# Sums of squares by ones times split parts, a summed last square, warm-up matmuls and a later epilogue in a two-layer decoder step

## The chip, the cores and the metric

The kernel runs on one core of a Trainium2 chip. The time is that of one execution on the device, in microseconds (us). The engines are PE (matrix products, with PEld for loading their stationary operand), DVE (vector operations), ACT (functions and copies), POOL and SP (the last two mostly issue transfers). Each works through its own row of instructions in order and waits on semaphores of the others.

## The reference

One step of a decoder trunk with two layers on 512 new tokens and 8 sequences of 4 tokens, 544 tokens of 1024 channels, all fp32:

```python
def rmsnorm(x, g):
    return x * lax.rsqrt(jnp.mean(x * x, axis=-1, keepdims=True) + EPS) * g

def trunk_layer(x, ...):
    x = x + 0.5 * swiglu(rmsnorm(x, g_ffn1), w_ffn1_up, w_ffn1_down)
    z = rmsnorm(x, g_mix) @ w_in
    ...                                   # three mixers: chunked gate, short convolution, pooling
    x = x + merged @ w_o
    x = x + 0.5 * swiglu(rmsnorm(x, g_ffn2), w_ffn2_up, w_ffn2_down)
    x = x + sigmoid(rmsnorm(x, g_ple) @ w_ple_gate) * (p @ w_ple_proj)
y = rmsnorm(x, g_final)
```

So there are four norms in a layer and one at the end, nine in all. The pooling mixer multiplies its output with a factor per channel (`c_scale`).

## The kernel before

**Data.** Channels lie on the 128 partitions, tokens along the free dimension: x is eight tiles of 128x544. A product of fp32 values is made of three PE passes over values split into a high and a low part in a reduced fp32 form (`split_to`: ACT copies the high part, DVE subtracts it for the low part). A matmul covers half of the tokens, 272 columns.

**Order of the work.** The program is written out as one stream, and each engine gets its instructions in the order of the source. Weights come in units of 128x512, which are loaded, added and split a few units ahead of their use. Each new unit calls `tick`, which also runs deferred steps: `later` is a list of steps with a number of ticks to wait, `background` a list that is spread over ticks, and `flush` runs all of both at once. PSUM has four tiles ps71 to ps74 of two banks, which `bank` and `ring_bank` hand out in turn by the counter `psi`.

**Products.** `gemm` (L303) is the plain form. `s_pair` (L326) computes two outputs with seven products on sums of blocks in place of eight; each of its products is 12 matmuls. It works in banks X, Y, Z, V: the products go to X, Y, X, Z, X, V, X, and X is copied out (L586, L588, L593) before it is filled again. A feed-forward (`ffn`, `ff_group`) makes its first output group by `gemm` (the program's very first four groups) and the others by `s_pair`. The epilogue of a plain group (`fin`) has the steps `e0` (gate times the norm's scale, L643), `dz` (Silu on ACT), `e1` (up times gate, L646), `dr`, `d2`, `d3`.

**Norms.** Each new block of x is squared on ACT and added to `acc` (`sumsq`, L385 to L389). While the products that follow already run on x without the scale, `rms_hooks` inserts the norm: `rms_sum` (L521) multiplies 128 tokens of `acc` at a time with a column of ones, which gives the sums as columns with a token per partition; DVE and ACT make the inverse root on these (`inv_sqrt`: Sqrt on ACT, the rest on DVE) and put them on diagonals (L528); `rms_bc` (L535) multiplies ones with the diagonals, which brings the scale to all partitions; ACT copies it to `rstd` (L537, L539). `RMS_AT` says after how many pieces of the first group of products (6 matmuls each) the two parts stand. Functions of ACT belong to tables, and a function of another table has an ACT_TABLE_LOAD ahead of it.

**End.** `ple_last` does the last sublayer in two parts of the tokens, blocks 0 to 1 and blocks 2 to 4 (256 and 288 columns), so that the first part's final norm and outputs lie under the second part's products (`gate`, `proj`: L1110). The last norm of all follows the last product.

Of the kernel before, what the change touches and what calls it, by code (L numbers as in the profile page):

```python
# [9 lines left out]
F32R = mybir.dt.float32r  # L10
# [33 lines left out]
N_PLAIN = 4  # L44
RMS_AT = 7, 14
V_TICKS = 9
RMS_AT0 = 8, 1
LAST_AT = 12, 26
TOK0 = T - P

GN_FFN1, GN_MIX, GN_FFN2, GN_PLE = range(4)
# [52 lines left out]
class Kern:  # L104
    def __init__(self, nc, ins, outs, sb, pp, plan=None):
        self.nc, self.ins, self.outs = nc, ins, outs
        self.sb = sb
        self.dry = plan is None
        self.seq, self.use = ([], [0]) if self.dry else plan
        self.used = 0  # L110
        self.held = ()
        self.keep = False
        self.extra = 0
        self.names = 0

# [9 lines left out]
        self.ones = self.mk([P, P], "ones")  # L125
        self.par = self.mk([P, PB_N], "par")
# [375 lines left out]
    def tok0(self, i):  # L502
        return i * P if i < 4 else TOK0

    def inv_sqrt(self, v, s, r, t):
        nc = self.nc
        nc.scalar.activation(s, v, AF.Sqrt)
        nc.vector.reciprocal(r, s)
        nc.vector.tensor_mul(t, r, r)
        nc.vector.tensor_mul(t, t, v)  # L510
        nc.vector.tensor_scalar(t, t, -0.5, 1.5, op0=ALU.mult, op1=ALU.add)
        nc.vector.tensor_mul(r, r, t)
# [4 lines left out]
    def rms_sum(self, ps, i0=0, i1=5):  # L517
        nc = self.nc
        for i in range(i0, i1):
            t0 = self.tok0(i)  # L520
            nc.tensor.matmul(ps[:, i:i + 1], self.acc[:, t0:t0 + P], self.ones[:, 0:1], start=True, stop=True)  # L521
        v, s, r, t = (self.cols[:, o + i0:o + i1] for o in (0, 8, 16, 24))
        nc.vector.tensor_scalar(v, ps[:, i0:i1], 1.0 / D, EPS, op0=ALU.mult, op1=ALU.add)
        self.inv_sqrt(v, s, r, t)
# [17 lines left out]
    def rms_hooks(self, then=None):  # L542
        st = {}
        start, self.start = self.start, False

        def first():
            st["ps"], = self.bank(1)
            self.rms_sum(st["ps"][:, 0, :])
            if start:
                self.later.append((RMS_AT0[1], second))  # L550

        def second():
            self.rms_bc(st["ps"])
            if then:
                self.background(*then)

        if start:
            self.later.append((RMS_AT0[0], first))
            return ()
        return tuple(zip(RMS_AT, (first, second)))  # L560

    def scaled(self, ps):
        t = self.slot()
# [40 lines left out]
    def ff_group(self, up, l, j, inp, first, plain, hs, hsl):  # L604
        nc = self.nc
        t_, o_ = self.slot(), self.slot()
        t, o = t_[0], o_[0]
        a, b = self.rpair()
        hi, lo = a[0][:, :], b[0][:, :]
        hs.append((hi, lo))  # L610
        hsl.extend((a, b))

        def dz():
            nc.scalar.activation(t[:, :], t[:, :], AF.Silu)  # L614

# [12 lines left out]

        def dr():
            nc.vector.tensor_mul(o[:, :], o[:, :], self.rstd[:, :])  # L630

        if plain:
            start = self.start
            xg = inp.tiles
            pg, pu = self.gemm([(up, l, j, xg, 0), (up, l, NFF + j, xg, 0)], kouter=first,
                               hooks=self.rms_hooks() if first else ())

            def s0():
                nc.scalar.activation(self.v2(t[:, :]), self.pv(pg), AF.Copy)
                nc.scalar.activation(self.v2(o[:, :]), self.pv(pu), AF.Copy)  # L640

            def e0():
                nc.vector.tensor_mul(self.v2(t[:, :]), self.pv(pg), self.v2(self.rstd[:, :]))  # L643

            def e1():
                nc.vector.tensor_mul(self.v2(o[:, :]), self.pv(pu), self.v2(t[:, :]))  # L646

            if start:
                fin = (s0,) + (None,) * (sum(RMS_AT0) - 5) + (d0, dz, d1, dr, d2, d3)
            else:  # L650
                fin = (e0, dz, e1, dr, d2, d3)
        else:
            r = self.rstd
            self.s_pair(up, l, NFF + j, j, inp.sets, o_, t_,
                        lambda out, ps: nc.vector.tensor_mul(out, ps, r[:, HT:]))
            nc.vector.tensor_mul(t[:, :HT], t[:, :HT], r[:, :HT])  # L656
            fin = (dz, dr, d1, d2, d3)
        self.later += [(1 + i, f) for i, f in enumerate(fin) if f]

    def ffn(self, l, which, inp, nxt, tail=None):  # L660
# [18 lines left out]
        for n in FF_PARTS:  # L679
            hs, hsl = [], []  # L680
            items = len(todo)
            for i in range(n):
                j = j0 + i
                self.extra = EXTRA[0] if j < plain else EXTRA[7]
                if j == plain:
                    self.flush()
                    self.drop(*inp.zs)
                self.ff_group(up, l, j, inp, j == 0, j < plain, hs, hsl)
# [39 lines left out]
    def mix(self, l, inp, nxt):  # L728
# [69 lines left out]
            self.split_later(b_, yb, yb_s, 1)  # L798

        self.extra = EXTRA[2]  # L800
        pc, px = self.gemm([W(Z_C), W(Z_XB)], kouter=True, hooks=self.rms_hooks(then=(steps, V_TICKS)))
        conv_in(0, self.scaled(pc), conv_x(0, px))
        def row(name):
            t = self.slot()
# [19 lines left out]
        def v_stat():  # L824
            cv = mv[:, :, 2]
            nc.vector.tensor_scalar_add(cv, mv[:, :, 1], EPS)
            self.inv_sqrt(cv, mv[:, :, 3], mv[:, :, 4], mv[:, :, 5])

        def v_norm(i):
            t = vt[i][:, :SEQ]  # L830
# [131 lines left out]
        def c_mix():  # L962
            for i, j in enumerate(reversed(range(G))):
                pc, = self.gemm([("c_w", l, 0, pooled[j], j)])
                t_ = self.slot()
                o = PB_CS + l * G + j
                nc.vector.tensor_scalar_mul(self.v2(t_[0][:, :]), self.pv(pc), self.par[:, o:o + 1])
                self.drop(*pooled_s[j])
                self.split_later(t_, yc, yc_s, 1 + i)
            yc.reverse()  # L970
# [124 lines left out]
    def ple_last(self, l, inp):  # L1095
# [35 lines left out]
        def proj(h, m):  # L1131
# [7 lines left out]
                nc.scalar.activation(self.acc[:, c], x, AF.Square)  # L1139
            else:  # L1140
                nc.scalar.activation(t, x, AF.Square)
                nc.vector.tensor_add(self.acc[:, c], self.acc[:, c], t)
            self.drop(t_)

        def norm_sum(h):
            rms[h], = self.bank(1)
            self.rms_sum(rms[h][:, 0, :], *parts[h])

        def norm_bc(h):
            self.rms_bc(rms[h], *parts[h])  # L1150

        def out(h, m):
            c = span(h)
# [24 lines left out]
        for m in range(KD):  # L1178
            if m + 1 < KD:
                gate(1, m + 1)  # L1180
            if m == 1:
                norm_sum(0)
            if m == 2:
                norm_bc(0)
            proj(1, m)
            if 2 <= m < 6:
                out(0, 2 * m - 4)
                out(0, 2 * m - 3)
        norm_sum(1)
        norm_bc(1)  # L1190
        for m in range(KD):
            out(1, m)

    def run(self):
        nc = self.nc
        nc.gpsimd.memset(self.ones[:, :], 1.0)
        nc.gpsimd.affine_select(self.ident[:, :], self.ones[:, :], pattern=[[1, P]], compare_op=ALU.is_equal,
                                fill=0.0, base=0, channel_multiplier=-1)
        def gain(l, which):
            return lambda m: self.gain(l, which, m)  # L1200

# [111 lines left out]
```

## Time and profile before

| | us |
|---|---|
| median of three runs | 2421.4 (2421.24 to 2422.02) |
| profiled execution, its time | 2421.51 |
| its span, first to last instruction | 2419.8 |
| PE busy in it | 2395.4 |
| mean granted clock of PE | 0.997 of full speed |

The span is what the trace covers; the execution's own time is 1.7 us longer. The views used below are the page's shares, the waits (who waited for whom), the chain (followed back from the last instruction to whatever released each step), the timeline (instructions in order of time, like ones merged), windows (busy time and clock in a stretch) and the groups by line. A record of an fp32 matmul appears twice, since PE runs it in two.

### The profile page before, as it was taken

What the parts mean: (1) busy time and instruction counts of PE and PEld (TensorE: products, weight loads), DVE (VectorE), ACT (ScalarE), POOL (GpSimd) and SP (SyncE); (2) the same over time, 40 slices, a digit from 0 to 9 for tenths busy, and PEclk for the clock granted to TensorE, in tenths of its full rate; (3) what the DMA queues carried; (4) which work ended last, traced back from release to release, by engine and by line L of the source; (5) the groups of instructions that cost most, each with busy time, mean ns of one, the idle gap of its engine ahead of it and who ended that gap; (6) DMA issues with size and microseconds to landing.
All of it is one profiled execution on the core that took longest, in us unless ns stands there. A gap on an engine that the chain in (4) does not pass through costs nothing.

```text
span 2419.8 us, 48050 instructions
## 1 busy us (share of the span) xinstructions
PE 2395.4 (99%) x18848; PEld 2381.8 (98%) x18848; DVE 1856.7 (77%) x3439; ACT 1208.4 (50%) x2355; POOL 225.6 (9%) x276
## 2 busy tenths in 40 slices
PE   8999999999999999999999999999999999999997
PEld 8999999999999999999999999999999999999997
DVE  7776777877878777778777777778779778867675
ACT  6444444655555544445554444556455555544452
POOL 1101000111100110100010110001111001101000
PEclk9999999999999999999999999999999999999998
DMA  6655561666554555555255554526565536556521
GB/s 205 143 146 140 145 170 40 176 151 153 145 140 121 140 147 147 146 139 160 60 142 135 145 155 126 166 63 173 137 157 154 161 79 153 154 126 154 145 75 38
DMA packets 180034, 329.78 MB, mean 136 GB/s; under 512 B 20256, under 2 KB 22560, under 8 KB 179808
## 3 DMA queue, kind: packets, MB, share of 16 engines
q1 hardware_dynamic: 141264, 255.92, 34.1%
q0 software_dynamic: 36672, 68.51, 16.9%
q8 instruction: 148, 2.42, 0.4%
q10 hardware_dynamic: 1872, 2.29, 0.3%
q14 instruction: 78, 0.64, 0.1%
HBM read 323.64 MB, written 2.99 MB: 135 GB/s over the span
## 4 chain that ended last, share of the span: by engine, by line
PE 97%; DVE 2%; ACT 1%; issue 0%; DMA 0%; DVEq 0%; ACTq 0%
PE ps L326 52%; PE ps L303 39%; PE ps L1110 2%; PE ps L846 2%; PE ps L535 0%; PE ps L521 0%; PE ps L995 0%; DVE s L250 0%; ACT L614 0%; DMA par<-in_par 0%; DVE s L1155 0%; DVE s L630 0%; DVE s L646 0%; PE ps L997 0%; DVE s L369 0%
## 5 line engine op out<-in xcount | busy, mean ns | idle before, releaser
L326 PE MATMUL ps<-s,s 128*128 128x272 f32 x10332 | 1311.2, 289 | 3.4 <-ACT s L586 1.9
L326 PEld LDWEIGHTS ps<-s,s 128*128 128x128 f32 x10332 | 1301.7, 189 | 5.2 <-ACT s L586 2.9
L303 PE MATMUL ps<-s,s 128*128 128x272 f32 x7536 | 962.7, 289 | 7.3 <-ACT s L448 7.3
L303 PEld LDWEIGHTS ps<-s,s 128*128 128x128 f32 x7536 | 952.2, 189 | 7.2 <-ACT s L448 7.2
L250 DVE TENSOR_TENSOR s<-s,s 128x512 fp32r<-128x512 f32 x1211 | 812.0, 685 | 20.1 <-ACT s L245 19.0
L245 ACT ACTIVATE s<-s 128x512 fp32r<-128x512 f32 x1211 | 705.2, 622 | 224.7 <-DVE s L238 222.2
L232 POOL DMA_DIRECT2D s<-in_wts x246 | 210.8, 877 | 1948.4 <-DMA s<-in_wts 717.0
L586 ACT ACTIVATE s<-ps 128x272 f32<-128x272 f32 x123 | 48.8, 397 | 461.7 <-PE ps L326 455.9
L669 DVE SCALAR_TENSOR_TENSOR x<-ps,x 128x544 f32<-128x544 f32 x128 | 92.7, 724 | 184.4 <-PE ps L303 182.6
L238 DVE TENSOR_TENSOR s<-s,s 128x512 f32<-128x512 f32 x246 | 168.6, 685 | 0.0
L589 DVE TENSOR_TENSOR s<-ps,s 128x272 f32<-128x272 f32 x123 | 54.3, 441 | 109.7 <-ACT s L588 109.1
L588 ACT ACTIVATE s<-ps 128x272 f32<-128x272 f32 x123 | 48.7, 396 | 100.4 <-PE ps L326 99.9
L593 ACT ACTIVATE s<-ps 128x272 f32<-128x272 f32 x123 | 48.6, 395 | 89.7 <-PE ps L326 89.4
L594 DVE TENSOR_TENSOR s<-ps,s 128x272 f32<-128x272 f32 x123 | 54.3, 441 | 49.5 <-ACT s L593 48.7
L620 ACT ACTIVATE s<-s 128x544 fp32r<-128x544 f32 x88 | 57.8, 657 | 37.2 <-DVE s L617 21.2
L888 DVE TENSOR_TENSOR s<-ps,s 128x544 f32<-128x544 f32 x48 | 34.8, 724 | 46.8 <-PE ps L303 43.2
L623 DVE TENSOR_TENSOR s<-s,s 128x544 fp32r<-128x544 f32 x88 | 63.4, 720 | 6.0 <-ACT s L620 5.8
L614 ACT ACTIVATE s<-s 128x544 f32<-128x544 f32 x88 | 57.8, 657 | 19.7 <-DVE s L656 18.0
L1110 PE MATMUL ps<-s,s 128*128 128x256 f32 (+1 forms) x480 | 63.2, 294 | 1.8 <-ACT rstd L537 1.8
L1110 PEld LDWEIGHTS ps<-s,s 128*128 128x128 f32 x480 | 62.0, 193 | 2.0 <-ACT rstd L537 2.0
L630 DVE TENSOR_TENSOR s<-s,rstd 128x544 f32<-128x544 f32 x88 | 63.4, 720 | 0.1
L617 DVE TENSOR_TENSOR s<-s,s 128x544 f32<-128x544 f32 x82 | 58.9, 719 | 0.4
(137 smaller groups left out, 1150.1 us busy)
## 6 DMA issues: line engine op xcount, KB each, us to landing
s<-in_wts SPq DMA_DIRECT2D x965, 256.0 KB, 3.3
s<-in_wts POOLq DMA_DIRECT2D x246, 256.0 KB, 5.1
x<-in_xT SPq DMA_DIRECT2D x4, 272.0 KB, 4.9
x<-in_xT ACTq DMA_DIRECT2D x4, 272.0 KB, 5.2
s<-in_pT POOLq DMA_DIRECT2D x4, 272.0 KB, 4.4
out_yT<-s SPq DMA_DIRECT2D x4, 144.0 KB, 1.8
out_yT<-s ACTq DMA_DIRECT2D x4, 144.0 KB, 1.8
s<-in_st_in POOLq DMA_DIRECT2D x2, 272.0 KB, 2.9
```

Of the source, the lines that this page charges most:

```text
L232: self.nc.gpsimd.dma_start(out=t, in_=src(1 if w == "R1" else 2, 4), accum_op=ALU.add)
L238: self.nc.vector.tensor_add(self.new_raw(w, u0, 2 if w == "R3" else 1), self.read_raw(a, u0), self.read_raw(b, u0))
L245: self.nc.scalar.activation(a[0][:, :UC], self.read_raw(w, u0), AF.Copy)
L250: self.nc.vector.tensor_sub(lo, self.read_raw(w, u0), hi.bitcast(F32))
L303: self.nc.tensor.matmul(ps[:, h, :HT], a, bh, start=first and i == 0, stop=last and i == 2)
L326: self.nc.tensor.matmul(ps, a, b, start=first and i == 0, stop=last and i == 2, skip_group_check=go_on)
L614: nc.scalar.activation(t[:, :], t[:, :], AF.Silu)
L617: nc.vector.tensor_mul(o[:, :], o[:, :], t[:, :])
L623: nc.vector.tensor_sub(lo, o[:, :], hi.bitcast(F32))
L630: nc.vector.tensor_mul(o[:, :], o[:, :], self.rstd[:, :])
L669: nc.vector.scalar_tensor_tensor(xm, self.pv(pst[i]), 0.5, xm, op0=ALU.mult, op1=ALU.add)
L1110: nc.tensor.matmul(ps, a, b[:, c], start=first and i == 0, stop=last and i == 2)
```

## The change

Seven norms take a new form. `norm_split` splits `acc` into high and low parts, `norm_sum` multiplies a full matrix of ones with both, so that the sums of squares come out on all partitions at once, and `norm_scale` makes the inverse root there: ACT's Abs_reciprocal_sqrt, then one correcting step (square on ACT, three operations on DVE). These are the norms of both feed-forwards but not of the mixers, of the gated embedding, and the final one: six in the first group of products, the last in two halves. The mixers' norms, which also need the scale as columns, keep the old form; there and in the layer norm Abs_reciprocal_sqrt replaces Sqrt and reciprocal. In the final norm's second half the last block's squares are not added to `acc`; a matmul of fp32 ones adds them in PSUM. Before the first products 14 matmuls of ones by ones run. The epilogue of the last plain group is queued after the flush, with a free step after `e0`, and runs during the next pair; `psi` moves on by three there. The pooling mixer's factor is applied by ACT.

```diff
-RMS_AT0 = 8, 1
-LAST_AT = 12, 26
+WARM = 14
+NORM_AT = 5, 11
+RMS_AT0 = 6, 3
+LAST_AT = 8, 19
...
-    def inv_sqrt(self, v, s, r, t):
-        nc = self.nc
-        nc.scalar.activation(s, v, AF.Sqrt)
-        nc.vector.reciprocal(r, s)
+    def inv_sqrt(self, v, r, t):
+        nc = self.nc
+        nc.scalar.activation(r, v, AF.Abs_reciprocal_sqrt)
...
+    def norm_split(self, c=slice(0, T)):
+        a, b = self.rpair()
+        self.split_to(self.acc[:, c], a[0][:, c], b[0][:, c])
+        return a, b
+
+    def norm_sum(self, split, outs, stop=True):
+        for ps, c in outs:
+            for i, t in enumerate(split):
+                self.nc.tensor.matmul(ps, self.ones_r[:, :], t[0][:, c], start=i == 0, stop=i == 1 and stop)
+        if stop:
+            self.drop(*split)
+
+    def norm_scale(self, ps, view=lambda ap: ap, c=slice(0, T)):
+        nc = self.nc
+        v_, u_ = self.slot(), self.slot()
+        v, u, r = (view(t[:, c]) for t in (v_[0], u_[0], self.rstd))
+        nc.scalar.activation(r, ps, AF.Abs_reciprocal_sqrt, bias=self.eps[:, :], scale=1.0 / D)
+        nc.vector.tensor_scalar(v, ps, -0.5 / D, -0.5 * EPS, op0=ALU.mult, op1=ALU.add)
+        nc.scalar.activation(u, r, AF.Square)
+        nc.vector.tensor_mul(u, u, v)
+        nc.vector.scalar_tensor_tensor(r, u, 1.5, r, op0=ALU.add, op1=ALU.mult)
+        self.drop(v_, u_)
...
-        return tuple(zip(RMS_AT, (first, second)))
+        return tuple(zip(RMS_AT if cols else NORM_AT, (first, second)))
...
+            if plain == 1:
+                self.flush()
+
...
             else:
-                fin = (e0, dz, e1, dr, d2, d3)
+                if first:
+                    self.psi += 3
+                fin = (e0, None, dz, e1, dr, d2, d3)
...
                 if j == plain:
-                    self.flush()
                     self.drop(*inp.zs)
...
-                nc.vector.tensor_scalar_mul(self.v2(t_[0][:, :]), self.pv(pc), self.par[:, o:o + 1])
+                nc.scalar.activation(self.v2(t_[0][:, :]), self.pv(pc), AF.Copy, scale=self.par[:, o:o + 1])
...
+                if h == 1 and m == KD - 1:
+                    return t_
                 nc.vector.tensor_add(self.acc[:, c], self.acc[:, c], t)
...
+            self.norm_sum(rms[h], [(ps, c)], last is None)
+            if last:
+                nc.tensor.matmul(ps, self.ones[:, :], last[0][:, c], start=False, stop=True)
...
-            proj(1, m)
+            last = proj(1, m)
+            if m == KD - 2:
+                norm_split(1)
...
+        warm, = self.bank(1)
+        for _ in range(WARM):
+            nc.tensor.matmul(warm[:, 0, :P], self.ones[:, :], self.ones[:, :], start=True, stop=True)
```

**ACT, the start of the first pair in layer 0's second feed-forward.** The names: ps_74 before and ps_71 after hold the norm, ps_71 is the pair's bank X in both, `rstd` the scale. Before:

```order
L537 ACTIVATE rstd<-ps_74 128x512
L539 ACTIVATE rstd<-ps_74 128x32
L614 ACT_TABLE_LOAD
L614 ACTIVATE s_1585_9987<-s_1585_9987 128x544
L620 ACTIVATE s_1587_9989<-s_1586_9988 128x544
L586 ACTIVATE s_1596_10136<-ps_71 128x272
L588 ACTIVATE s_1597_10137<-ps_71 128x272
```

After, at the same place:

```order
L561 ACT_TABLE_LOAD
L561 ACTIVATE rstd<-ps_71,eps 128x544
L563 ACTIVATE s_1601_10087<-rstd 128x544
L620 ACTIVATE s_1602_10126<-ps_71 128x272
L622 ACTIVATE s_1603_10127<-ps_71 128x272
L648 ACT_TABLE_LOAD
L648 ACTIVATE s_1588_9993<-s_1588_9993 128x544
```

The two copies of X (L586 and L588, now L620 and L622) have moved ahead of the Silu and its table load (L614, now L648); the epilogue's split stands further on.

**DVE, the last two blocks of the final norm's second part.** Here x_69 and x_70 are the blocks, `cols` the columns of sums. Before:

```order
L1142 TENSOR_TENSOR acc<-acc,s_4677_30414 128x288
L1136 TENSOR_TENSOR s_4680_30457<-ps_74,s_4680_30457 128x288
L1137 TENSOR_TENSOR x_70<-x_70,s_4680_30457 128x288
L1142 TENSOR_TENSOR acc<-acc,s_4680_30457 128x288
L523 TENSOR_SCALAR cols<-ps_71 128x3
L508 RECIPROCAL cols<-cols 128x3
...
L528 TENSOR_SCALAR s_4681_30490<-ident,cols 128x128 x2
L528 TENSOR_SCALAR s_4681_30490<-ident,cols 128x32
L1155 SCALAR_TENSOR_TENSOR s_4682_30499<-x_63,par,rstd 128x288
```

After:

```order
L1182 TENSOR_TENSOR acc<-acc,s_4698_30366 128x288
L348 TENSOR_TENSOR s_4703_30423<-acc,s_4702_30422 128x288
L1174 TENSOR_TENSOR s_4701_30409<-ps_72,s_4701_30409 128x288
L1175 TENSOR_TENSOR x_70<-x_70,s_4701_30409 128x288
L562 TENSOR_SCALAR s_4704_30438<-ps_73 128x288
L564 TENSOR_TENSOR s_4705_30439<-s_4705_30439,s_4704_30438 128x288
L565 SCALAR_TENSOR_TENSOR rstd<-s_4705_30439,rstd 128x288
L1201 SCALAR_TENSOR_TENSOR s_4706_30445<-x_63,par,rstd 128x288
```

The low part of the split (L348) now stands between the sixth addition to `acc` and the last block's product; the last addition, the column steps and the diagonals are gone, and three operations of 288 columns stand ahead of the outputs.

## Rows read from the trace of the kernel before

**Rows 1.** The page: busy time by engine; shares of the chain.

```profile
PE 2395.4 (99%) x18848; PEld 2381.8 (98%) x18848; DVE 1856.7 (77%) x3439; ACT 1208.4 (50%) x2355; POOL 225.6 (9%) x276
...
PE 97%; DVE 2%; ACT 1%; issue 0%; DMA 0%; DVEq 0%; ACTq 0%
```

**Rows 2.** Waits of PE: line, releaser: us in total, times, longest.

```profile
PE ps L303 <- ACT s L448: 7.3, 1, 7.3
...
PE ps L326 <- ACT s L586: 1.9, 3, 0.7
...
PE ps L1110 <- ACT rstd L537: 1.8, 1, 1.8
PE ps L326 <- DVE s L967: 1.4, 2, 0.7
```

**Rows 3.** Chain through layer 0's second feed-forward norm: start, us, what.

```profile
781.04 1.01 PE ps L521 x10
...
787.42 1.05 PE ps L535 x10
...
789.19 1.28 ACT L614
...
790.49 0.67 ACT s L614
...
791.17 0.73 DVE s L646
```

**Rows 4.** Chain: the first products, and a stretch of plain products.

```profile
7.27 23.13 PE ps L303 x168
...
346.27 41.34 PE ps L303 x330
```

**Rows 5.** Windows of PE at the start: length, busy, matmuls touched, granted clock.

```profile
8.00:9.00 1.00, 1.00 (x7) 1.00 1.04 405
12.00:13.00 1.00, 1.00 (x10) 1.00 1.06 406
```

**Rows 6.** A window of PE in the last stage, same columns.

```profile
2387.00:2391.00 4.00, 4.00 (x21) 0.57 0.21 70
```

**Rows 7.** Groups by line and form: count, busy us, mean ns, idle before.

```profile
L346 ACT ACTIVATE s<-x,par 128x544 fp32r<-128x544 f32 x32 | 24.0, 751 | 44.8 <-DVE x L669 44.4
...
L639 ACT ACTIVATE s<-ps 128x544 f32<-128x544 f32 x1 | 0.6, 599 | 0.0
```

**Rows 8.** Timeline of DVE ahead of that norm (start, us).

```profile
778.72 1.55 DVE L389 TENSOR_TENSOR acc<-acc,s 128x544 f32<-128x544 f32 x2
...
783.15 0.44 DVE L467 TENSOR_TENSOR s<-s,s 128x272 f32<-128x272 f32 x1
```

**Rows 9.** Timeline of the first pair after it.

```profile
793.69 5.54 PE L326 MATMUL ps<-s,s 128*128 128x272 f32 x42 [0.65 <-ACT s L586]
795.50 0.40 ACT L588 ACTIVATE s<-ps 128x272 f32<-128x272 f32 x1 [1.87 <-PE ps L326]
...
797.50 0.43 DVE L591 TENSOR_TENSOR s<-ps,s 128x272 f32<-128x272 f32 x1
```

**Rows 10.** Timeline of POOL at the start.

```profile
0.81 0.20 POOL L1196 MEMSET ones<- 128x128 f32 x1 [0.29 <-POOLq L1291]
```

**Rows 11.** Chain at the end.

```profile
2404.11 0.47 DVE s L1136
...
2406.93 0.45 ACT s L1141
...
2407.91 1.46 PE ps L521 x6
...
2413.21 0.52 DVE s L1155
```

**Rows 12.** Timeline where the third branch is scaled, layer 0.

```profile
670.43 1.14 ACT L245 ACTIVATE s<-s 128x512 fp32r<-128x512 f32 x2
670.87 2.85 DVE L967 TENSOR_SCALAR s<-ps,par 128x544 f32<-128x544 f32 x4
```

More of the change, by code (lines that the diff above doesn't have):

```diff
@@ L125, in __init__ @@
         self.ones = self.mk([P, P], "ones")
+        self.ones_r = self.mk([P, P], "ones_r", F32R)
+        self.eps = self.mk([P, 1], "eps")
         self.par = self.mk([P, PB_N], "par")
@@ L521, in rms_sum @@
             nc.tensor.matmul(ps[:, i:i + 1], self.acc[:, t0:t0 + P], self.ones[:, 0:1], start=True, stop=True)
-        v, s, r, t = (self.cols[:, o + i0:o + i1] for o in (0, 8, 16, 24))
+        v, r, t = (self.cols[:, o + i0:o + i1] for o in (0, 16, 24))
         nc.vector.tensor_scalar(v, ps[:, i0:i1], 1.0 / D, EPS, op0=ALU.mult, op1=ALU.add)
-        self.inv_sqrt(v, s, r, t)
+        self.inv_sqrt(v, r, t)
         self.diag = self.slot()
@@ L540, in rms_bc, with rms_hooks @@
         self.drop(self.diag)
-    def rms_hooks(self, then=None):
+    def norm_split(self, c=slice(0, T)):
[18 more added lines that the diff above has]
+        self.drop(v_, u_)
+    def rms_hooks(self, then=None, cols=False):
         st = {}
@@ L547, in first @@
             st["ps"], = self.bank(1)
-            self.rms_sum(st["ps"][:, 0, :])
+            if cols:
+                self.rms_sum(st["ps"][:, 0, :])
+            else:
+                st["split"] = self.norm_split()
             if start:
@@ L552, in second @@
         def second():
-            self.rms_bc(st["ps"])
+            if cols:
+                self.rms_bc(st["ps"])
+            else:
+                ps = st["ps"]
+                self.norm_sum(st["split"], [(ps[:, h, :HT], slice(h * HT, (h + 1) * HT)) for h in range(2)])
+                self.norm_scale(self.pv(ps), self.v2)
             if then:
@@ L630, in dr @@
             nc.vector.tensor_mul(o[:, :], o[:, :], self.rstd[:, :])
-        if plain:
+        if plain > 0:
             start = self.start
@@ L685, in ffn @@
                 if j == plain:
-                    self.flush()
                     self.drop(*inp.zs)
-                self.ff_group(up, l, j, inp, j == 0, j < plain, hs, hsl)
+                self.ff_group(up, l, j, inp, j == 0, plain - j, hs, hsl)
                 while len(todo) > items * (n - 1 - i) // n:
@@ L800, in mix @@
         self.extra = EXTRA[2]
-        pc, px = self.gemm([W(Z_C), W(Z_XB)], kouter=True, hooks=self.rms_hooks(then=(steps, V_TICKS)))
+        pc, px = self.gemm([W(Z_C), W(Z_XB)], kouter=True, hooks=self.rms_hooks((steps, V_TICKS), True))
         conv_in(0, self.scaled(pc), conv_x(0, px))
@@ L826, in v_stat @@
             nc.vector.tensor_scalar_add(cv, mv[:, :, 1], EPS)
-            self.inv_sqrt(cv, mv[:, :, 3], mv[:, :, 4], mv[:, :, 5])
+            self.inv_sqrt(cv, mv[:, :, 4], mv[:, :, 5])
         def v_norm(i):
@@ L1141, in proj, with norm_split, norm @@
                 nc.scalar.activation(t, x, AF.Square)
+                if h == 1 and m == KD - 1:
+                    return t_
                 nc.vector.tensor_add(self.acc[:, c], self.acc[:, c], t)
             self.drop(t_)
[L1145 to L1150, printed above, removed]
+        def norm_split(h):
+            rms[h] = self.norm_split(span(h))
+        def norm(h, last=None):
+            pst, = self.bank(1)
+            c = span(h)
+            ps = pst[:, 0, :c.stop - c.start]
+            self.norm_sum(rms[h], [(ps, c)], last is None)
+            if last:
+                nc.tensor.matmul(ps, self.ones[:, :], last[0][:, c], start=False, stop=True)
+                self.drop(*rms[h], last)
+            self.norm_scale(ps, c=c)
         def out(h, m):
@@ L1180, in ple_last @@
                 gate(1, m + 1)
+            if m == 0:
+                norm_split(0)
             if m == 1:
-                norm_sum(0)
-            if m == 2:
-                norm_bc(0)
-            proj(1, m)
+                norm(0)
+            last = proj(1, m)
+            if m == KD - 2:
+                norm_split(1)
             if 2 <= m < 6:
@@ L1188, in ple_last @@
                 out(0, 2 * m - 3)
-        norm_sum(1)
-        norm_bc(1)
+        norm(1, last)
         for m in range(KD):
@@ L1198, in run @@
                                 fill=0.0, base=0, channel_multiplier=-1)
+        nc.gpsimd.memset(self.eps[:, :], EPS)
+        nc.vector.tensor_copy(self.ones_r[:, :], self.ones[:, :])
         def gain(l, which):
```

## The prediction

> **What bounds the kernel now.** I began with the engine shares [rows 1]: PE, the matmul engine, is busy for 2395.4 of the 2419.8 us of the span, and the chain that ended last is PE for 97%. So only two things can change the time much: what PE executes, and when it stands still or runs slowly. ACT, DVE and the transfers bound nothing as long as PE does not wait for them. The second view was PE's waits outside the last microseconds [rows 2]: four kinds, 12.4 us together, and each belongs to a place that the change touches. Third, the chain, for what PE spends on a norm [rows 3] and on its normal work [rows 4]. Last came the two ends of the program, where the rate and the clock show slow stretches [rows 5, 6], and the places where work moves between engines [rows 7 to 12].
>
> The unit of account: the chain has 330 matmuls of 128x272 in 41.34 us [rows 4], 0.125 us each. A weight unit of 24 matmuls is 3.0 us, a product of a pair (12 matmuls) 1.51 us.
>
> **Six norms inside the first group (of seven that change).** In one such norm PE spends 1.01 us on the column sums and 1.05 us on the broadcast [rows 3]. The change takes both away and puts in four matmuls of ones by split halves, of the shape of the normal ones: 4 x 0.125 = 0.50 us. That is 1.55 us less (1.56 by these rows), six times: **-9.3 us**. The mixer's two norms keep the old form. The chain to the scale also gets other links, but off PE: on ACT the root from PSUM (0.60 us, by the plain copy of PSUM [rows 7]) and a square (about 0.65 us, as the Silu of that size [rows 3]), on DVE two more passes of about 0.75 us (two additions take 1.55 [rows 8]); with a table load of 1.28 us [rows 3] some 4.0 us. It hides behind the five pieces of the group that follow the sum, 5 x 6 x 0.125 = 3.8 us, and then behind the first product, which does not need the scale. Without that cover it would cost up to 4 us a norm.
>
> What is late next: the sum now reads the split of the accumulated squares. In layer 0's second feed-forward the last two additions to them end at 778.72 + 1.55 = 780.27 [rows 8]. The split's low half stands on DVE behind an operation that starts at 783.15 and lasts 0.44 us [rows 8], so it ends near 784.3. The group began at 781.04 - 42 x 0.125 = 775.8, so its sum falls after 66 matmuls at 784.05, and the second matmul, which reads the low half, at 784.2. I book +0.1 us for each of the two second feed-forwards: **+0.2**. The other norms have 0.3 us or more to spare by the same reckoning.
>
> **First pairs after a plain group.** Before, the flush stands behind the epilogue, so ACT must finish table load, Silu and split before it empties the pair's first bank (L586); PE's third product waits for that, three times, 1.9 us in all [rows 2]. Now the bank is emptied first. But the epilogue is stretched over the products, and the third step of it (Silu, with its table load) stands behind the copy of the third product's bank; the up half's product (L646 before, L683 after) follows, and the sixth product needs the bank that this reads. From layer 0's second feed-forward as it ran: the third product starts at 793.69, that copy ends at 795.50 + 0.40 [rows 9], then 1.28 us of load and 0.66 of Silu [rows 3] end at 797.85, DVE is free at 797.50 + 0.43 by its row [rows 9], and the 0.72 us of the product [rows 3] end at 798.6. The sixth product would start at 793.69 + 3 x 1.51 = 798.2. So about 0.4 us of waiting comes back: three times -0.65 + 0.4, **-0.7**. Bounds: nothing comes back (-1.9), or DVE has one more split of 0.68 us in front (+0.1).
>
> **Start.** PE's first matmul waits until 7.27 us for ACT [rows 2, 4]. It then touches 7 matmuls in a microsecond against 10 later [rows 5]: 168 matmuls take 23.13 us [rows 4] where 168 x 0.125 = 21.0, and some 0.2 of the rest is the last one's drain. So 1.9 us go to a slow stretch. Its counts look like those of the last stage at a granted clock of 0.57 [rows 6], so I read it as the lower level, 1.2 GHz, although the column says 1.00 here. The 14 warm-up matmuls can begin when the ones are there, at 0.81 + 0.20 [rows 10]. Priced as the column sums, 28 records at 0.10 us make 2.9 us; at the late sums' rate (6 records in 1.46 us [rows 11]) 6.8 us, less some drain. They so fill the wait, to between 4 and 7.6 us. I take it that the clock is then up and stays up to 7.27; a DVE split that is needed at the sixth matmul gives back 0.1: **-1.75**. Bounds: -1.9, and +0.3 (no effect, and a late end).
>
> **Last norm, first half.** Sums and broadcast of two blocks are 4 of 10 records each, 0.4 x (1.01 + 1.05) = 0.8 us; two matmuls of 256 columns, 0.24 us, replace them: **-0.6**. The broadcast's bank is what PE waits 1.8 us for (the scale's copy, L537 [rows 2]), because ACT has first to load Sigmoid's table. The new form writes its bank once, and it is read about 3 us before its next user: **-1.8**. From 2387 to 2391 the granted clock is 0.57 [rows 6]: it fell to its lower level, 1.2 GHz, after PE had stood still for that wait, and 0.43 x 2 x 4 us = 3.4 us at half rate lost **-1.7**, which goes with the wait.
>
> **Tail.** Let the sixth block's last PSUM product start at zero (2404.11). Its product, its addition, its square on ACT and the addition of that end at 1.92, by 0.47 us for a step on DVE and 0.45 for one on ACT. Before, the last block's same four steps follow, PE sums at 3.80, and the outputs start at 9.10 [rows 11]. After, DVE's row has the low half of the split ahead of the last block: ACT's half ends near 2.4, DVE's at 2.9, the last block's product and addition at 3.8, its square at 4.25. Then the table load, 1.28 us [rows 3], ends at 5.5; beside it runs the fp32 matmul of 288 columns. No row has that shape; by the late sums (0.24 us a record) its two records take 0.5 us, and 1.1 if they grow with the columns from 128 to 288. Both stay under the load. Root 0.45, square 0.45, two passes of 0.5 on DVE: the outputs start at 7.5. **-1.6** (bounds -0.7, if the matmul outlasts the load by 0.9, and -2.2).
>
> **Scale of the third branch, on ACT.** PE waits 0.7 us, twice, for the first of four DVE scales (L967 [rows 2]), which starts at 670.87 in a row of 2.85 us [rows 12]. On ACT the first stands behind the first of two weight splits that begin at 670.43 [rows 12], so starts near 671.0 and lasts 0.60 (plain copy of PSUM) to 0.75 us (copy with a scale per partition) [rows 7]: PSUM is free at 671.65, as before. **0.** Bounds: -0.7 and +0.6, both layers. The Trainium skill speaks against this move: "ScalarE: Activation LUTs", Rules for kernel authors, sends multiplications to VectorE. The row gives DVE 0.71 us for each of the four in their stream, so ACT is at most equal; by the figures of the same page (What ACT_TABLE_LOAD costs) I estimate 0.73 us.
>
> **The sum**: -9.3 + 0.2 - 0.7 - 1.75 - 0.6 - 1.8 - 1.7 - 1.6 = -17.25 us. The profiled execution took 2421.51 us (span 2419.8 and 1.7 around it), within 0.1 of the median: 2404.2 us, **0.7% faster**. A measurement of this kernel tells 0.2%, 4.8 us, from no change.
>
> **Rivals.**
> - *The warm-up brings nothing*: the clock does not rise on these matmuls, or falls again before 7.27. Against the forecast speaks that PE may stand still for a microsecond or more before 7.27, and that the clock fell after 1.8 us in the last stage; for it, that it did not fall after the waits of 0.7 us. 2406.0.
> - *The clock falls in the last stage all the same*, after another wait there. DVE is blocked for 3 us by the new chain, with four banks of slack. 2405.9.
> - *ACT's scale is slow*: four at 0.75 us and a split push the emptying of the next pair's first bank 0.3 us past the third product, in each layer. 2404.8. This is what the rule of that page would bring here.
> - *Waits grow*: an extra DVE split before the sixth product and before each sum, 0.5 us at nine places. 2408.
> - *Given back*: each norm holds DVE for some 3 us, with weight splits queued behind. They are made four units, 12 us, ahead, which speaks against it; if that cover were thin, 2 us at six norms is 12 us: 2416.6, no change that shows.
> - *Slower*: the sum matmul waits in PE's row for the low half. If DVE brings it over 2 us late, the clock falls after each wait as in the last stage, and six norms cost 6 x (2.2 + 1.7) = 23.4 us: 2427.6. It decides from 2.0 us of lateness; I reckon 0.1.
>
> **Numbers.** The forecast as summed 0.55 (2402.5 to 2406 alone, from the bounds of its terms); no warm-up 0.15; clock falls late 0.10; slow ACT scale 0.06; grown waits 0.07; given back 0.04; slower 0.03. All but the last two are over 0.2% faster: 0.93. To hold eight in ten with the bounds of start, tail and pairs, 2401 to 2408.5.
>
> **What the next profile would show.** Right: PE 9 to 10 us less busy in its norms; column sums gone except in the mixers; ten matmuls a microsecond from 7.3 us on; a granted clock of 1.00 until PE's last matmul; PE waits of about 0.4 us on the up half's product in place of those on L586; outputs that start 7.5 us after the sixth block's last product. Wrong would be: long PE waits on the split of the squares, a clock of 0.5 anywhere before the tail, or a norm of over 0.6 us on PE.

## The result, and the profile after

The changed kernel takes **2404.35 us** (median of 6 runs, 2404.25 to 2404.9) where the kernel before takes 2421.32 (6 runs, 2419.03 to 2422.02): a ratio of 0.9932, 95% interval 0.992 to 0.9945. The forecast was 2404.2. The profiled spans are 2419.8 and 2402.5 us, so 17.3 us are to be found; the lines shown stand 3 to 53 further on in the new kernel than in the old.

The page's busy times, which answer to [rows 1]:

```profile
PE 2386.7 (99%) x18766; PEld 2371.2 (99%) x18766; DVE 1854.3 (77%) x3376; ACT 1221.5 (51%) x2364; POOL 225.5 (9%) x277
```

PE is busy for 8.7 us less, although the warm-up has added 5.8. The waits of PE, all of them, which answer to [rows 2]:

```profile
PE ps L553 <- ACT s L347: 1.7, 1, 1.7
PE ps L330 <- ACT s L1005: 1.4, 2, 0.7
PE ps L1267 <- POOL ones L1243: 1.1, 1, 1.1
PE ps L1194 <- ACT s L1179: 0.9, 1, 0.9
PE ps L330 <- DVE s L683: 0.6, 3, 0.2
PE ps L553 <- DVE s L348: 0.4, 2, 0.3
PE ps L307 <- ACT s L452: 0.3, 1, 0.3
PE ps L307 <- DVE s L683: 0.2, 1, 0.2
```

The wait for the first operands (7.3) is filled, those on L586 and L537 are gone. New are short ones on the up half's product (L683) and on the low half of the split of the squares (L348); that on the third branch's scale has changed its engine and kept its size. The two on L347 and L1179 lie in the tail.

PE's timeline at the start, and at layer 0's second feed-forward (start, length, what, how often, idle time ahead); the first two rows answer to [rows 4], the others to [rows 3, 9]:

```profile
1.07 5.83 PE L1267 MATMUL ps<-ones 128*128 128x128 f32 x28 [1.07 <-POOL ones L1243]
7.23 24.45 PE L307 MATMUL ps<-s,s 128*128 128x272 f32 x192 [0.34 <-ACT s L452]
31.53 0.66 PE L553 MATMUL ps<-s,ones_r 128*128 128x272 f32 x4
32.03 12.20 PE L307 MATMUL ps<-s,s 128*128 128x272 f32 x96
...
780.40 1.05 PE L553 MATMUL ps<-s,ones_r 128*128 128x272 f32 x4
781.29 3.94 PE L307 MATMUL ps<-s,s 128*128 128x272 f32 x30
785.06 7.66 PE L330 MATMUL ps<-s,s 128*128 128x272 f32 x60
792.95 34.91 PE L330 MATMUL ps<-s,s 128*128 128x272 f32 x276 [0.23 <-DVE s L683]
```

Such rows are read by their starts, since the end of one overlaps the next: the first norm takes 32.03 - 31.53 = 0.50 us, the one at 780 takes 0.89, and from 785.06 the 60 matmuls of five products take 7.89 us where 60 x 0.1253 is 7.52, so the sixth comes 0.37 us late. Behind a wait the second matmul is late too, by another 0.1 us: 0.23 us behind the first in place of 0.125. The start as windows (length, busy, matmuls touched, granted clock), which answers to [rows 5]:

```profile
7.50:8.00 0.50, 0.50 (x6) 1.00 1.01 396
8.00:9.00 1.00, 1.00 (x9) 1.00 1.06 410
```

Full rate from 7.5 us on. The tail, by the chain (start, length, what):

```profile
2388.07 0.47 DVE s L1174
...
2392.34 1.34 PE ps L1194 x2
...
2393.71 0.51 ACT rstd L561
...
2395.79 0.52 DVE s L1201
```

From the sixth block's product to the outputs 7.72 us, where [rows 11] give 9.10. One piece is larger than booked: the fp32 matmul of the last squares, 1.34 us. The windows of PE there:

```profile
2392.00:2393.00 1.00, 0.66 (x2) 0.56 0.00 0
2393.00:2394.00 1.00, 0.68 (x2) 0.50 0.00 0
```

So the granted clock does still fall once, behind waits of 1.70 and 0.94 us, just under that matmul.

### The profile page after: what moved, and what is told of

It reads as the page before. It is cut to its first block, busy times and chain, and to the rows that moved or that the text cites. A ratio compares the mean times of both kernels' runs of the same rounds, so it can differ in the third digit from the quotient of the medians.

```text
span 2402.5 us, 47828 instructions
## 1 busy us (share of the span) xinstructions
PE 2386.7 (99%) x18766; PEld 2371.2 (99%) x18766; DVE 1854.3 (77%) x3376; ACT 1221.5 (51%) x2364; POOL 225.5 (9%) x277
## 4 chain that ended last, share of the span: by engine, by line
PE 91%; DVE 5%; ACT 3%; issue 1%; DMA 0%; SPq 0%; DVEq 0%; ACTq 0%
PE ps L330 53%; PE ps L307 32%; PE ps L1148 2%; PE ps L884 2%; DVE s L254 1%; ACT s L452 1%; ACT s L430 1%; DVE s L491 1%; ACT s L249 1%; DVE acc L393 1%; ACT s L392 0%; PE ps L1033 0%; DVE s L469 0%; DVE s L470 0%; DVE s L462 0%
## 5 line engine op out<-in xcount | busy, mean ns | idle before, releaser
L620 ACT ACTIVATE s<-ps 128x272 f32<-128x272 f32 x123 | 48.9, 398 | 463.7 <-PE ps L330 448.9
L622 ACT ACTIVATE s<-ps 128x272 f32<-128x272 f32 x123 | 48.8, 397 | 103.3 <-PE ps L330 102.4
L648 ACT ACTIVATE s<-s 128x544 f32<-128x544 f32 x88 | 57.7, 656 | 20.5 <-DVE s L695 18.5
```

## The experiments

All times below stand against the changed kernel's 2404.35 us unless something else is said. The kernel before, run beside the three groups of experiments, took 2421.73, 2419.18 and 2421.04 us (medians; single runs from 2418.88 to 2422.7), so differences of a few tenths of a microsecond are read from the traces and not from medians.

**Without the warm-up, and with four matmuls** (there the new line is `WARM = 4`).

```diff
-WARM = 14
+WARM = 0
```

> The changed kernel without its 14 warm-up matmuls. Theory (the slow stretch at the start is the lower clock level, and the warm-up moves it into PE's idle time): the first products touch 6 to 7 matmuls in a microsecond again until about 11.3 us, and the time is 1.7 us longer, 2406.0 us. Rival (the slow stretch had another cause, such as late operands, and something else in the change removed it): the rate stays at 9 to 10 from 8 us on, 2404.3 us.

> Four warm-up matmuls in place of 14, so that PE stops near 2.8 us and stands still for over 4 us before its first product. Theory (what counts is PE's work right up to the first product): as without warm-up, 2406.0 us. Rival (any first use of PE is enough): as with 14, 2404.3 us.

Measured: 2406.44 us without (2405.17 to 2406.73), 2405.96 with four (2405.33 to 2406.25). PE's windows without:

```profile
12.00:13.00 1.00, 1.00 (x6) 1.00 1.06 399
13.00:14.00 1.00, 1.00 (x8) 1.00 1.03 371
14.00:15.00 1.00, 1.00 (x10) 1.00 1.04 391
```

The slow stretch is back and lasts until 13.6 us or so (before: 11.3), with four matmuls until 12. PE then stood still for 4.0 us before its first product, and the early matmuls were worth nothing on the rate there. That the warm-up removes the stretch is shown: it is gone with 14 matmuls and there with 0 and 4, in size near the forecast. That it is the clock's lower level is read from the rate alone, 6 to 7 matmuls in a microsecond as at 0.50 elsewhere. What the four lacked is not shown: all their records stand 0.21 us apart, while those of the fourteen come 0.21 us apart up to 6.1 us and 0.11 from 6.3, so with fourteen the rate rises before the first product, and with four it never rose. Whether a longer warm-up that ended 4 us early would have kept it is not shown. The column says 1.00 throughout, so at the start the rate is to be read from the count of matmuls. The runs also lie closer together with it: over 0.65 us in the changed kernel, 1.6 without warm-up, 3.0 in the kernel before.

**The six norms in the old form.**

```diff
-RMS_AT0 = 6, 3
-LAST_AT = 8, 19
+RMS_AT0 = 8, 1
+LAST_AT = 12, 26
...
     def rms_hooks(self, then=None, cols=False):
-        st = {}
+        cols, st = True, {}
```

> The six norms of a first group of products back in the old form (columns of sums, diagonals, broadcast) at their old places; the final norm, the warm-up, the late epilogue and the scale on ACT stay as changed. Theory (the norms are the largest term and add to the others): PE loses 2.15 to 2.25 us at each norm in place of 0.5 to 1.04, in all 8.8 us more, 2413.1 us. Rival (what the norms save on PE is partly given back as waits elsewhere, so that undoing it costs less): 2410 us or under.

Measured: 2413.87 us (2413.16 to 2414.96), 9.5 us more. The norms are the largest term. By the starts in the profiled execution the five later norms cost 1.2 to 1.75 us more each, just what the new form saves there, so nothing of that is given back elsewhere. What goes beyond the 8.8 is at the first norm:

```profile
35.01 1.30 PE L538 MATMUL ps<-s,ones 128*128 128x128 f32 x10 [1.42 <-DVE s L531]
```

PE now comes to the column sums ahead of it 1.0 us sooner (29.22 for 30.24 us), and DVE's diagonals are late: this norm costs 3.75 us more, 2.0 beyond what the others do. The kernel before has no such wait, so the 9.5 us are more than what the norms save. The profiled execution is the longest of the seven (2414.96 us), and how long the wait was in the others is open.

**The early flush.**

```diff
-            if plain == 1:
-                self.flush()
...
-                if first:
-                    self.psi += 3
-                fin = (e0, None, dz, e1, dr, d2, d3)
+                fin = (e0, dz, e1, dr, d2, d3)
...
                 if j == plain:
+                    self.flush()
                     self.drop(*inp.zs)
```

> The epilogue of the last plain group flushed before the next pair, as in the kernel before, with the rest of the change. Theory (the third product then waits 0.8 us in place of 0.38 us at the sixth, three times; in the first feed-forward a wait of 0.39 us goes and 0.4 us come back in the first pair): 1.3 us more, 2405.6 us; by the prediction's term 0.7 us more, 2405.1 us. Rival (the scale is now ready so early that the old order costs nothing): 2404.3 us.

Measured: 2411.55 us (2411.18 to 2411.98), 7.2 us more: outside all three expectations. PE at the pair of [rows 9]:

```profile
788.44 1.77 PE L330 MATMUL ps<-s,s 128*128 128x272 f32 x12 [0.72 <-DVE s L677]
791.63 39.39 PE L330 MATMUL ps<-s,s 128*128 128x272 f32 x312 [1.42 <-ACT s L620]
```

and what ACT and DVE do ahead of it:

```profile
785.69 0.72 DVE L565 SCALAR_TENSOR_TENSOR rstd<-s,rstd 128x544 f32<-128x544 f32 x1
...
787.67 0.71 DVE L677 TENSOR_TENSOR s<-ps,rstd 128x544 f32<-128x544 f32 x1
788.42 0.66 ACT L648 ACTIVATE s<-s 128x544 f32<-128x544 f32 x1 [2.36 <-DVE s L677]
...
790.63 0.66 ACT L654 ACTIVATE s<-s 128x544 fp32r<-128x544 f32 x1 [1.55 <-DVE s L664]
791.19 0.38 ACT L620 ACTIVATE s<-ps 128x272 f32<-128x272 f32 x1
```

The new norm's scale is ready only at 786.41. The epilogue (gate times scale, Silu, split) stands in ACT's row ahead of the copy of the first bank (L620), so this comes at 791.19 and the third product waits 1.42 us for it; the second waits 0.72 us for the bank that the gate half (L677) still reads. That is 0.72 + 1.42 us at each of three pairs, and 1.27 us in the first feed-forward: 7.6 us of idle time on these lines, where the changed kernel has 0.8 on L683. So the new norm needs the later epilogue. The edit also takes back the shift of the banks (`psi`), and no run parts the two: of the waits, the 0.72 us are for a bank, the 1.42 us for the order in ACT's row.

**Old norms and early flush together**, the two edits above in one kernel.

> Old norms and early flush together; warm-up, new final norm and scale on ACT stay. Undone alone, the norms cost 9.5 us and the flush 7.2 us. Theory (the two parts hang together: the early flush costs so much only since the new chain to the scale is longer and stands before it; with the old norms it costs what it did before): 2413.9 + 1.3 = 2415.2 us. Rival (the flush has a cost of its own, whatever the norm): 2413.9 + 7.2 = 2421.1 us.

Measured: 2415.32 us (2414.98 to 2416.09), with the wait of [rows 2] on the pair's first bank back as it was:

```profile
PE ps L330 <- ACT s L620: 1.9, 3, 0.6
```

The two parts hang together: the early flush costs 7.2 us beside the new norms and 1.5 beside the old. Put the other way, the new norms are worth 9.5 us with the late epilogue and 3.8 with the early one; in both the old form carries late diagonals at the first norm (waits of 1.42 and 1.26 us).

**The sum earlier, and later** (there the new line is `NORM_AT = 5, 12`).

```diff
-NORM_AT = 5, 11
+NORM_AT = 5, 8
```

> The sum of the squares three pieces (2.25 us) earlier in the first group, with the split of the squares where it was, so that PE waits for the split's low half on purpose: 2.6 to 2.8 us at the three norms at 781, 1208 and 1969 us, 0.9 us at the one at 1147 us; the norms at 31 and 2335 us are not touched. Theory of the prediction's slower rival (the clock falls after each wait of over 2 us, as it did after 1.76 us in the last stage of the kernel before): 7.7 us of waits and 3 x 1.7 us at the lower level, 2417 us. Rival (the clock stays up, since PE is busy before and behind): 2412 us.

> The sum of the squares one piece (0.75 us) later than in the changed kernel, at all norms of that rule. Theory (three of the norms lose 0.39, 0.42 and 0.54 us because DVE splits the squares late, and the scale has time to spare): these 1.35 us go, 2403.0 us. Rival (the scale, 0.75 us later, delays the up half's product, and the sixth product of the next pair waits longer by as much): 3 x 0.75 - 1.35 = 0.9 us more, 2405.3 us.

Measured: 2414.79 us for the early sum (2413.21 to 2416.49), 2403.03 for the later one (2402.79 to 2403.22). The early sum, PE's timeline at 779 us and its windows there:

```profile
779.12 0.39 PE L553 MATMUL ps<-s,ones_r 128*128 128x272 f32 x1 [0.51 <-ACT s L347]
781.11 1.05 PE L553 MATMUL ps<-s,ones_r 128*128 128x272 f32 x3 [1.61 <-DVE s L348]
781.96 7.31 PE L307 MATMUL ps<-s,s 128*128 128x272 f32 x48
789.11 7.66 PE L330 MATMUL ps<-s,s 128*128 128x272 f32 x60
```

```profile
781.00:782.00 1.00, 0.89 (x4) 0.51 0.00 0
782.00:783.00 1.00, 1.00 (x6) 0.50 0.00 0
...
784.00:785.00 1.00, 1.00 (x8) 0.78 0.00 0
```

The clock falls to 0.50 behind the wait, in the middle of a busy program: the three matmuls of the sum from 781.11 take 0.85 us where they take 0.48 behind the two waits that follow, and the 48 from 781.96 take 7.15 in place of 6.0. At 1213 and 1977 us, behind the same 1.60 us, those 48 take 7.55 and 7.52; at 1150, behind 0.78 us, the clock stays at 1.00. A fall costs 1.5 us at each of the three, a little under the 1.7 of the forecast. So the first theory's mechanism is there, and the profiled execution, at 2416.49 us, comes close to its 2417. It is the longest of the runs, though, and the median lies between the two expectations: the mean granted clock is 0.996 in the two longest runs and 0.997 in the other six, and whether the clock fell three times in those is open.

The later sum brings the 1.3 us that were expected:

```profile
781.43 0.66 PE L553 MATMUL ps<-s,ones_r 128*128 128x272 f32 x4
781.93 3.15 PE L307 MATMUL ps<-s,s 128*128 128x272 f32 x24
```

The four matmuls take 0.50 us here and at the other three norms (1147.98, 1208.54, 1968.83), and no wait at a pair behind them has grown, so the scale has the time. (The wait on L683 in the first feed-forward, which the edit does not touch, is 0.6 us in this trace and 0.2 in the changed kernel's: places differ by that much without a cause in the program.)

**The up half scaled early.**

```diff
             def e1():
-                nc.vector.tensor_mul(self.v2(o[:, :]), self.pv(pu), self.v2(t[:, :]))
+                nc.vector.tensor_mul(self.v2(o[:, :]), self.pv(pu), self.v2(self.rstd[:, :]))
...
-                fin = (e0, None, dz, e1, dr, d2, d3)
+                fin = (e0, e1, dz, None, d1, d2, d3)
```

> In the epilogue of a plain group the up half is multiplied with the norm's scale out of PSUM one step behind the gate half, and the product of the two comes after the Silu; the operations are as many as before. Theory (the sixth product waits for the up half's bank, which stands behind table load and Silu): the waits of 0.38 us at three pairs and 0.39 us in the first feed-forward go, 1.5 us less, 2402.8 us. Rival (DVE is late there with its other work, and another read of PSUM takes its place): 2404.3 us.

Measured: 2402.26 us (2402.19 to 2402.6), 2.1 us less. No wait on L683 is left in the trace, at the three pairs or in the first feed-forward. The theory stands. Most of the 0.6 us beyond it is the second matmul behind each wait, late by 0.1 us: by the starts in the two traces the four places win 0.49, 0.50, 0.47 and 0.46 us, 1.9 in all, where the expectation had 0.38 and 0.39.

**The third branch's scale back on DVE.**

```diff
-                nc.scalar.activation(self.v2(t_[0][:, :]), self.pv(pc), AF.Copy, scale=self.par[:, o:o + 1])
+                nc.vector.tensor_scalar_mul(self.v2(t_[0][:, :]), self.pv(pc), self.par[:, o:o + 1])
```

> The scale of the third branch back on DVE, with the rest of the change. Theory (the bank becomes free at the same moment on either engine, since both have other work ahead of the first of the four): PE waits as long, no change, 2404.3 us. Rival (multiplications belong on DVE, as the Trainium skill's page ScalarE: Activation LUTs has it in its Rules for kernel authors): PE's two waits of 0.85 us shrink, down to 2402.7 us.

Measured: 2404.16 us (2404.07 to 2405.13), no difference that shows. The first scale, what stands ahead of it, and PE's wait, with ACT (the changed kernel, first) and with DVE:

```profile
666.99 0.62 ACT L249 ACTIVATE s<-s 128x512 fp32r<-128x512 f32 x1
667.51 2.51 ACT L1005 ACTIVATE s<-ps,par 128x544 f32<-128x544 f32 x4
...
668.25 2.02 PE L330 MATMUL ps<-s,s 128*128 128x272 f32 x14 [0.67 <-ACT s L1005]
```

```profile
667.31 0.68 DVE L254 TENSOR_TENSOR s<-s,s 128x512 fp32r<-128x512 f32 x1
...
667.91 2.85 DVE L1005 TENSOR_SCALAR s<-ps,par 128x544 f32<-128x544 f32 x4
...
668.75 1.54 PE L330 MATMUL ps<-s,s 128*128 128x272 f32 x10 [0.67 <-DVE s L1005]
```

Four scales take 2.51 us in ACT's row and 2.85 in DVE's. The rule of the Trainium skill, "ScalarE: Activation LUTs", Rules for kernel authors, which sends multiplications to VectorE with a figure for bf16, gets no support here: DVE is not the faster of the two for these scales of fp32 out of PSUM. On either engine a weight split stands just ahead of the first scale, and the wait is the same.

**The tail**, with and without eight matmuls of ones ahead of the last squares (the loop of eight is left out in the second kernel).

```diff
-                if h == 1 and m == KD - 1:
+                if h == 1 and m >= KD - 2:
                     return t_
...
             if last:
+                for _ in range(8):
+                    nc.tensor.matmul(pst[:, 1, :P], self.ones[:, :], self.ones[:, :], start=True, stop=True)
-                nc.tensor.matmul(ps, self.ones[:, :], last[0][:, c], start=False, stop=True)
+                for t in last:
+                    nc.tensor.matmul(ps, self.ones[:, :], t[0][:, c], start=False, stop=t is last[-1])
...
+            if m == KD - 2:
+                nc.scalar.activation(self.cols[:, 0:1], self.eps[:, :], AF.Abs_reciprocal_sqrt)
...
-            if m == KD - 2:
+            if m == KD - 3:
                 norm_split(1)
```

> Only the tail: the last two blocks' squares are added by fp32 matmuls, so that the split of the squares is done before the last product; a one-element root is placed behind the last Sigmoid, so that the table is loaded before it is needed; and eight matmuls of ones by ones between the split's sum and the two fp32 matmuls keep PE working. Theory (the tail is held by the table load and by the fp32 matmul, which runs at the lower clock level because PE stood still before it): the two fp32 matmuls take some 0.7 us each in place of 1.33 and the root starts about 2.3 us earlier, 2402.0 us. Rival (1.33 us is what 288 columns cost at any level): the two take 2.7 us, no more than 1 us is won, 2403.3 us or over.

> The same tail without the eight matmuls of ones. Theory (lower clock level behind PE's idle time): two fp32 matmuls of 1.33 us in a row, the root 1.0 us earlier than in the changed kernel, 2403.3 us. Rival (the level has no part in it): the same time as with the eight matmuls.

Measured: 2402.81 us with the eight (2402.6 to 2403.27), 2402.72 without (2402.41 to 2403.27); from the sixth block's product to the outputs 5.9 and 5.8 us in place of 7.72. Without them, PE and the table load:

```profile
2389.06 1.28 ACT L1230 ACT_TABLE_LOAD   x1
2389.07 0.43 PE L553 MATMUL ps<-s,ones_r 128*128 128x288 f32 x2
...
2390.94 1.24 PE L1195 MATMUL ps<-s,ones 128*128 128x288 f32 x4 [1.44 <-ACT s L1179]
2392.22 0.50 ACT L561 ACTIVATE rstd<-ps,eps 128x288 f32<-128x288 f32 x1 [0.99 <-PE ps L1195]
```

```profile
2391.00:2392.00 1.00, 1.00 (x4) 1.00 0.00 0
```

Two fp32 matmuls of 288 columns (four records) take 1.24 us together, from the start of the first to the end of the last, against 1.34 for one alone in the changed kernel at a granted clock of 0.5 to 0.56. The root starts 3.7 to 3.8 us after the sixth block's product in place of 5.6, 1.8 to 1.9 us earlier where 2.3 were expected with the eight. So the size of 1.34 us was the clock's lower level (1.2 GHz), as the first theory had it; but its other half, that PE has to be kept working, fell: with the split moved ahead PE stands still for 1.44 us only, the clock stays at 1.00, and there is nothing for the eight matmuls to keep up. The 1.6 us come from the earlier split, the hidden table load and the clock together; no run here parts the first two.

**All three at once**: the later sum, the early up half, and the tail with the eight matmuls.

> Three edits on top of the change: the sum one piece later (measured alone: 1.3 us less), the up half scaled out of PSUM early (2.1 us less), and the tail with the eight matmuls (2.3 us less expected). Theory (they lie at different places and add): 5.7 us less, 2398.6 us. Rival (the later sum makes the scale late for the early product of the up half, which now needs it): the waits at three pairs come back by up to 0.75 us each, 2400.9 us.

Measured: 2399.18 us (2398.94 to 2399.25), a ratio of 0.991 to the kernel before, interval 0.9895 to 0.9925; 5.2 us less than the changed kernel. The single gains as measured, 1.3 + 2.1 + 1.5 = 4.9, add up; the expectation was 0.6 us off because it had the tail at 2.3. Beside the wait for the ones at the start one is left on PE, that on the third branch's scale:

```profile
PE ps L330 <- ACT s L1005: 1.4, 2, 0.7
```

## Why the prediction was right, step by step

The measured column is worked out from starts on PE's row in the two profiled executions: for the same matmul of the program, by how much the changed kernel is ahead before and behind each place. Only where a place has two entries are they parted, by the rate of the matmuls around (0.1253 us for 272 columns, 0.132 for 288).

| step | predicted us | measured us |
|---|---|---|
| start | -1.75 | -1.7 |
| six norms on PE | -9.3 | -10.4 |
| waits for the split's low half | +0.2 | +1.35 |
| first pairs after a plain group | -0.7 | -1.2 |
| last stage: sums, wait, clock | -0.6 - 1.8 - 1.7 | -0.7 - 2.0 - 1.5 |
| tail | -1.6 | -1.4 |
| third branch's scale | 0 | 0 |
| elsewhere, small shifts | | +0.3 |
| sum | -17.25 | -17.3 |

- **Six norms.** The rows [rows 3] undersize the old norm, since after column sums and after the broadcast the next matmuls lose about 0.1 us each: between 780.88 and 789.88 us, 54 normal matmuls and a norm took 9.00 us, so the norm 2.23, not 2.06. The new one costs 0.50 where nothing is late.
- **Waits for the low half.** Here a term was mis-sized: 0.39 us at 780, 0.42 at 1208 and 0.54 at 1969 in place of 0.1 twice. The place at 780 was found, and DVE's time right: forecast 784.3, which is 780.8 in the new trace, and measured 780.75 by the first of these rows:

```profile
780.03 0.72 DVE L348 TENSOR_TENSOR s<-acc,s 128x544 fp32r<-128x544 f32 x1
```

```profile
780.88 1.17 PE L521 MATMUL ps<-ones,acc 128*128 128x1 f32 x10
```

What failed is PE's time. The second row, of the kernel before, has the column sums at 780.88; the 781.04 of [rows 3], from which the prediction counted, is the start of a piece of the chain, so the sum was put 0.16 us too late. The second matmul then came 0.28 us late in place of 0.1, and the third another 0.1. That at 1208 was not seen at all ("0.3 us or more to spare"). The later sum confirms the cause.
- **First pairs.** The mechanism came as forecast: the sixth product is 0.37 us late (forecast 0.4), with the loss of the matmul behind it 0.48. What goes is 0.9 us at each pair, not 0.65: the idle time in a row leaves out the drain of the matmul before (0.15 us) and the same loss of 0.1 behind the wait. Not foreseen: 0.49 us on L683 in the first feed-forward, offset there by 0.39 us in its first pair. The experiment with the early flush shows more: this term was priced on its own, as if the new norms stood without it. Beside them the moved epilogue is worth 7.2 us, the cover without which the prediction's "up to 4 us a norm" would have been paid in part.
- **Start.** Right in size by the two runs with fewer warm-up matmuls, and the rate bears out the cause; but its size differs from trace to trace: the slow stretch ended at 11.3, 12 and 13.6 us in those of three kernels.
- **Last stage.** Right: no wait and a granted clock of 1.00 in it up to the tail.
- **Tail.** The fp32 matmul was put under the table load with 0.5 to 1.1 us and took 1.34, at the lower clock; the load ends at about the same time, so that cost little. Of the signs that the prediction named, "1.00 until PE's last matmul" was wrong, and one of its signs of being wrong came: three norms took over 0.6 us on PE (0.89, 0.92 and 1.04 us).
- **Third branch's scale.** Right: PE waits 0.67 us where it waited 0.70, and one scale on ACT takes 0.70 to 0.73 us by its record, as estimated.
- **Rivals.** *Slower* did not come, and its mechanism is real: low halves as late as in the early-sum run cost the wait and a fall of the clock. *Waits grow* came in part, at three norms and on L683. *Given back* would have come in size, at 7.2 us, had the epilogue stayed where it was, though by another path than weight splits that queue on DVE. *No warm-up effect* and *slow ACT scale* are refuted by their experiments. Two rivals' times do not follow from their own terms (nine times 0.5 us gives 2408.7, six times 2 us 2416.2); no chance hangs on that.

The mechanisms were right, but the total is nearer than the terms deserve, and that is luck: +1.15 us of unforeseen waits and +0.5 us in the tail and elsewhere stood against -1.1 at the norms and -0.5 at the pairs.

## What to carry to other kernels

Read a stall's cost from the starts of the same matmul, not from the idle time in its row; the drain, the late second matmul behind a wait and the cost of changing from one kind of matmul to another are missing there. When one part of a change lengthens a chain and another moves its consumer, price them together: here undoing the norms costs 9.5 us and undoing the moved epilogue 7.2, but undoing both 11.0. Some of PE's waits have a second price behind them, the lower clock, which cost 1.5 us a time in the middle of the program, so a wait behind which the clock falls is worth shortening first.

## What the runs showed of the hardware

- The granted clock fell to 0.5 behind PE waits of 1.61 us (with 0.51 just before), of 1.60 us (0.20 and 0.42 before), of 1.70 and then 0.94 us, and of 1.76 us, and not behind 1.44, 0.78 or 0.7 us. After the fall 48 matmuls of 272 columns took 7.15 to 7.55 us in place of 6.0.
- At the program's start the column gives 1.00 while matmuls run at 6 to 7 in a microsecond, as they do at 0.50 later (6).
- Two fp32 matmuls of 288 columns with a 128x128 operand took 1.24 us together at a granted clock of 1.00; one alone took 1.34 at 0.50 to 0.56.
- A matmul right behind a wait is followed 0.23 us later in place of 0.125 (780.81 and 781.03 us, 792.95 and 793.18 us in the changed kernel).
- A table load took 1.28 us in every row shown, and in the changed kernel the one that starts at 781.05 us stands 0.02 us behind the instruction before it, with the next 0.01 us behind its end. The Trainium skill, "ScalarE: Activation LUTs" (What ACT_TABLE_LOAD costs), gives the same 1283 ns for the load, and with a drain about 2.66 us for every switch to a different set. No drain shows in these rows; the measurement decides.
